# The head of the first FFN in a two-layer trunk, built another way

## The chip, the cores and the metric

The kernel runs on one core of one Trainium2 chip, alone. The metric is the device time of one execution in microseconds (us), taken as the median of three runs. An execution's profile gives a span, from the first to the last instruction of the core.

## What is computed

Six sublayers in a row (FFN, mixer, FFN, twice) update x, which has 256 rows of 1024. Each begins with a norm whose shift and scale come from a linear layer on c (`mod`), and the change touches the very first one and the first part of its FFN. Cut to that:

```python
c_act = jax.nn.silu(c)                                    # 1 x 1024
mod = (c_act @ mod_w[i] + mod_b[i]).reshape(B, 3, 3, 1024)
def adaln(x, g, shift, scale):
    return rmsnorm(x, g) * (1 + scale) + shift
def swiglu(h, w_in, w_out):                               # w_in: 1024 x 5632
    gate, up = jnp.split(h @ w_in, 2, axis=-1)
    return (jax.nn.silu(gate) * up) @ w_out
h = adaln(x, norm_g[i, 0], mod[:, 0, 0], mod[:, 0, 1])    # shift, scale
x = x + 0.5 * mod[:, 0, 2] * swiglu(h, ffn_w_in[i, 0], ffn_w_out[i, 0])
```

## The kernel before

Everything is float32. A product h @ w is done in three matmul passes per tile on TensorE: h and w are each split into a rounded high part and a rest (`hTh` and `hTl`, `hl[:, 0]` and `hl[:, 1]`), and high x high, high x rest and rest x high are added in PSUM. For a weight tile of 128 rows (one K tile, of 8) ScalarE makes the high part (a cast) and VectorE the rest (a subtraction); h stands transposed (1024 on partitions in 8 K tiles, 256 columns), and its two halves of 128 rows are t = 0 and 1.

**The head** (function `head`, lines 427 to 534) makes the first h and the first products with it: `g` (the first 1024 columns of the gate, four PSUM banks) and `u00a` (the first 512 columns of up, two banks). After it comes `u00b`, the next 512 columns of up, a plain `product`, then `g001` and the rest of the FFN. Shift (part 0) and scale (part 1) of layer 0 each need c_act times a 1024 x 1024 block of `mod_w`. The head does this in four blocks of 256 columns per part, 1 MB each (`hw`, or `spare`, which borrows a buffer that is not needed yet). Of the eight K slices of a block, `NPE` are multiplied on TensorE with `cb` as the stationary operand, that is c_act spread over all 128 columns, so that the result stands on every row; the others are summed on VectorE into `mb` (line 472), and a matmul with `ones` adds that sum (line 477). A matmul with a single row brings in the bias `mod_b` (line 462). Shift and scale are then rows: VectorE forms x * r * scale + shift in two steps (lines 485, 487), r being 1/rms of the row, TensorE transposes the block (line 494), and ScalarE and VectorE make `hTh` and `hTl`.

**Order.** Loads go out on the SP queue in the order of the code, as soon as their buffer is free; at most eight are on the way, since a load waits for the one eight places before it. SP stops at a load whose buffer is still read, and all later loads wait behind it. On the other engines a scheduler sorts the instructions by its own estimates of time; an engine then runs its list strictly in order. `hw` has two buffers (tag `mraw`), the transposed blocks and dummy results share two PSUM banks (tag `tr`).

## Time and profile before

| what | value |
| --- | --- |
| median of three runs (lowest, highest) | 1153.16 us (1152.34, 1154.13) |
| the profiled execution: time, span | 1151.26 us, 1149.5 us |
| busy: TensorE, its weight loads, VectorE, ScalarE | 98%, 82%, 72%, 51% |
| DMA, mean over the span | 244 GB/s |
| chain that ended last: TensorE, VectorE, ScalarE | 88%, 6%, 2% |

A float32 matmul shows as two records (passes) in the trace, one with the operands of the split products (float32r) as one. The busy time of TensorE is modelled from the starts of pipelined passes, so a gap between starts tells more than a duration does. "PEclk" is the clock that was granted to TensorE, as a share of its upper level; "<-" in brackets names what ended a wait.

### The profile page before, as it was taken

The page shows a single profiled execution, that of the slowest core. Times are in us where ns is not written, and L with a number is a line of the kernel's source. Part 1 is how long each engine was busy: PE and PEld are TensorE (multiplying, and loading weights), DVE is VectorE, ACT ScalarE, POOL GpSimd, SP SyncE. Part 2 cuts the span into 40 slices and gives each one's busy share as a digit, 9 for nine tenths or more (in the row PEclk, how much of TensorE's full clock was granted, in tenths as well). Part 3 has the DMA queues.
Part 4 walks back from the last instruction along what each step waited for, and adds up shares of the span by engine and source line. Part 5 has one row for each costly group of instructions (what it writes and reads, how often), then busy time and mean ns, then how long its engine had stood idle before and what let it go on. Part 6 is the DMA issues. An engine that isn't in the chain of part 4 may idle for free.

```text
span 1149.5 us, 14007 instructions
## 1 busy us (share of the span) xinstructions
PE 1125.9 (98%) x5381; PEld 943.8 (82%) x5381; DVE 828.0 (72%) x1008; ACT 590.8 (51%) x849; POOL 32.2 (3%) x42
## 2 busy tenths in 40 slices
PE   6999999999999999999999999999999999999997
PEld 5788998887878888888988788898877778889985
DVE  3887787845698788694678858577898877644653
ACT  3365454437555554554544546354457666544541
POOL 0000000010000000000000000000000000000000
PEclk9999999999999999999999999999999999999999
DMA  9787897547687685775778558487877555455640
GB/s 337 273 347 277 287 336 284 219 165 256 226 337 290 246 327 205 277 262 178 272 269 331 184 206 306 140 308 271 311 242 289 202 183 200 166 183 151 219 144 37
DMA packets 86538, 279.99 MB, mean 244 GB/s; under 512 B 4980, under 2 KB 15284, under 8 KB 86472
## 3 DMA queue, kind: packets, MB, share of 16 engines
q1 hardware_dynamic: 86472, 279.10, 68.5%
q8 instruction: 42, 0.69, 0.2%
q14 instruction: 24, 0.20, 0.1%
HBM read 278.01 MB, written 1.07 MB: 243 GB/s over the span
## 4 chain that ended last, share of the span: by engine, by line
PE 88%; DVE 6%; ACT 2%; DMA 1%; issue 1%; POOL 1%; SPq 0%; POOLq 0%; DVEq 0%; ACTq 0%
PE ps_o L201 27%; PE ps_g L201 19%; PE ps_u L201 19%; PE ps_v L201 5%; PE ps_gu L201 4%; PE ps_qk L201 3%; PE ta L386 2%; PE mps L132 1%; PE ps_vv L201 1%; PE hps L465 1%; DVE hl_g L180 1%; PE ps_u00b L201 1%; PE sv L609 1%; PE ps_u00a L201 1%; POOL rx L273 1%
## 5 line engine op out<-in xcount | busy, mean ns | idle before, releaser
L201 PE MATMUL ps_o<-hl_o,ahl 128*128 128x512 f32 x1440 | 333.9, 391 | 1.0 <-ACT ahl L342 1.0
L201 PEld LDWEIGHTS ps_o<-hl_o,ahl 128*128 128x128 f32 x1440 | 269.0, 188 | 56.3 <-ACT ahl L342 1.2
L201 PE MATMUL ps_g<-hl_g,hTh 128*128 128x512 f32 (+1 forms) x768 | 203.5, 375 | 0.7 <-ACT hTh L498 0.7
L180 DVE TENSOR_TENSOR hl_o<-raw_o,hl_o 128x1024 fp32r<-128x1024 f32 x120 | 145.7, 1222 | 53.8 <-ACT hl_o L179 53.2
L179 ACT CAST hl_o<-raw_o 128x1024 fp32r<-128x1024 f32 x120 | 125.6, 1055 | 112.2 <-PE ps_o L201 73.6
L201 PE MATMUL ps_u<-hl_u,hTh 128*128 128x512 f32 (+1 forms) x704 | 181.5, 369 | 0.0
L114 DVE SCALAR_TENSOR_TENSOR ma<-mw,cs,ma 128x1024 f32<-128x1024 f32 x128 | 163.8, 1280 | 13.4 <-DMA mw<-in_mod_w_dram 12.7
L201 PEld LDWEIGHTS ps_g<-hl_g,hTh 128*128 128x128 f32 x768 | 141.5, 189 | 21.7 <-ACT hTh L498 1.4
L180 DVE TENSOR_TENSOR hl_g<-raw_g,hl_g 128x1024 fp32r<-128x1024 f32 (+1 forms) x96 | 107.6, 1132 | 55.2 <-ACT hl_g L179 54.9
L201 PEld LDWEIGHTS ps_u<-hl_u,hTh 128*128 128x128 f32 x704 | 129.6, 188 | 17.6
L179 ACT CAST hl_g<-raw_g 128x1024 fp32r<-128x1024 f32 (+1 forms) x96 | 91.9, 980 | 100.4 <-PE ps_u L201 86.8
L180 DVE TENSOR_TENSOR hl_u<-raw_u,hl_u 128x1024 fp32r<-128x1024 f32 (+1 forms) x88 | 98.5, 1127 | 61.6 <-ACT hl_u L179 60.4
L201 PE MATMUL ps_g<-hl_g,hTl 128*128 128x512 f32 (+1 forms) x384 | 121.4, 377 | 0.0
L179 ACT CAST hl_u<-raw_u 128x1024 fp32r<-128x1024 f32 (+1 forms) x88 | 85.5, 974 | 61.0 <-PE ps_g L201 55.9
L201 PE MATMUL ps_u<-hl_u,hTl 128*128 128x512 f32 (+1 forms) x352 | 108.6, 369 | 0.0
L201 PEld LDWEIGHTS ps_g<-hl_g,hTl 128*128 128x128 f32 x384 | 71.4, 189 | 11.2 <-issue 1.3
L201 PEld LDWEIGHTS ps_u<-hl_u,hTl 128*128 128x128 f32 x352 | 65.4, 188 | 8.7
L201 PE MATMUL ps_gu<-hl_gu,hTh 128*128 128x512 f32 x192 | 55.0, 394 | 0.0
L201 PE MATMUL ps_v<-hl_v,hTh 128*128 128x512 f32 x192 | 54.2, 392 | 0.3 <-ACT hl_v L179 0.3
L180 DVE TENSOR_TENSOR hl_v<-raw_v,hl_v 128x1024 fp32r<-128x1024 f32 x24 | 28.9, 1220 | 27.3 <-ACT hl_v L179 27.3
L201 PEld LDWEIGHTS ps_v<-hl_v,hTh 128*128 128x128 f32 x192 | 35.8, 188 | 8.3 <-ACT hl_v L179 0.5
L201 PEld LDWEIGHTS ps_gu<-hl_gu,hTh 128*128 128x128 f32 x192 | 35.8, 188 | 7.1
(160 smaller groups left out, 1202.0 us busy)
## 6 DMA issues: line engine op xcount, KB each, us to landing
mw<-in_mod_w_dram SPq DMA_DIRECT2D x64, 1024.0 KB
raw_o<-in_ffn_w_out_dram SPq DMA_DIRECT2D x44, 1024.0 KB
raw_g<-in_ffn_w_in_dram SPq DMA_DIRECT2D x32, 1024.0 KB
raw_u<-in_ffn_w_in_dram SPq DMA_DIRECT2D x28, 1024.0 KB
raw_g<-in_ffn_w_in_dram SPq DMA_DIRECT2D x16, 768.0 KB
...
```

What stands on the lines that cost most here:

```text
L114: nc.vector.scalar_tensor_tensor(st["acc"], w[:, j, :], cs[:, k0 + j:k0 + j + 1], st["acc"], op0=ALU.mult, op1=ALU.add)
L132: nc.tensor.matmul(ps, lhs, hl[:, j, sl], start=j == 0, stop=j == 1)
L179: nc.scalar.copy(hl[:, 0, :w], r[:, kt % 2, :w])
L180: nc.vector.tensor_sub(hl[:, 1, :w], r[:, kt % 2, :w], hl[:, 0, :w].bitcast(F32))
L201: nc.tensor.matmul(ps[t, h][:, :cw], lhs(k, t)[p], hls[k][:, wp, o:o + cw], start=k == 0 and p == 0 and wp == 0, stop=k == nk - 1 and p == 1)
L273: nc.gpsimd.tensor_tensor(r, m, mhalf, op=ALU.pow)
L386: nc.tensor.transpose(ps[:, j * P:(j + 1) * P], src[:, j * P:(j + 1) * P], ident)
L465: nc.tensor.matmul(ps[part], cb[:, k, :], w[:, k, :], start=False, stop=k == KD - 1)
L609: nc.tensor.matmul(sv[:, sl], wsT[:, g, :], v[n][:, t, lo - n * D:hi - n * D], start=True, stop=True)
```

## The change

- Shift and scale are no longer spread over rows. The stationary operand is `cz`, 32 columns of which only the first holds c_act; eight K slices (or four, `HPE`) go to four strips of 32 output partitions, strip k mod 4 for slice k (`tile_position`). For blocks 3 and 4 VectorE adds the other four slices onto that PSUM tile. One matmul per 128 columns, with the summed tile as stationary operand and a single column of ones, sums over partitions and leaves shift and scale with their index on the partition (`columns`, `hv`).
- x, times r, is transposed at once (`xT`), before shift and scale are known. h is then one ScalarE instruction per K tile with scale and bias taken per partition (`acts_hi`), and its rest needs a second one and one on VectorE (`acts_lo`). `mod_b` and `norm_g` come in as 24 rows and are transposed in one go (`vrow`, `base`).
- The blocks are five (128, 128, 256, 256 and 256 columns), shift and scale side by side. Weights of `g` and `u00a` are loaded K tile by K tile, not in pairs, and x goes first in the queue.
- TensorE, VectorE and ScalarE keep the order of the code in the head (`manual_schedule`), with 33 dummy matmuls (`fill`) in it, 16 of them at the start.

```diff
-NPE = ((6, 5), (5, 2), (3, 1), (2, 1))
+BLOCKS = ((0, 128), (128, 128), (256, 256), (512, 256), (768, 256))
+HPE = (8, 8, 8, 4, 4)
...
+        def load(k):
+            for n, c0, w in (("g", 0, D), ("u", FF, 512)):
...
+                nc.sync.dma_start(raw[n][:, k % 2, :], w_in[k * P:(k + 1) * P, c0:c0 + w])
...
         def modulation(b):
...
+            n = 2 * BLOCKS[b][1]
+            ps = tr_bank(f"hps{b}")
+            for k in range(HPE[b]):
+                q = k % 4 * 32
+                nc.tensor.matmul(ps[q:q + 32, :n], cz[:, k, :], weight(b, k), start=k < 4,
+                                 stop=k >= HPE[b] - 4, tile_position=(0, q),
+                                 skip_group_check=True)
...
+        def gather(b):
...
+            if HPE[b] == KD:
+                nc.vector.tensor_copy(mb[:, :n], ps[:, :n])
+            prev = ps
+            for k in range(HPE[b], KD):
+                nc.vector.scalar_tensor_tensor(mb[:, :n], weight(b, k), cs[:, k:k + 1],
+                                               prev[:, :n], op0=ALU.mult, op1=ALU.add)
+                prev = mb
...
+        def columns(b):
+            ps, mb = sums[b]
+            for j in range(2 * BLOCKS[b][1] // P):
+                nc.tensor.matmul(ps[:, j:j + 1], mb[:, j * P:(j + 1) * P],
+                                 ones.bitcast(F32)[:, 0:1], start=True, stop=True)
+        def vectors(b):
...
+            nc.vector.tensor_add(v, sums[b][0][:, :2 * nj].rearrange("p (a j) -> p a j", a=2),
+                                 base[:, 0:2, k0:k0 + nj])
+            nc.vector.tensor_mul(v[:, 1, :], v[:, 1, :], base[:, 2, k0:k0 + nj])
...
+        def acts_hi(k):
+            sh, sc = hv[:, 0, k:k + 1], hv[:, 1, k:k + 1]
+            hi = hT["hi"][:, k, :]
+            nc.scalar.activation(hi, xT[k // 4][:, k % 4, :], AF.Identity, scale=sc, bias=sh)
+            less[k] = half_tile(f"hm{k}")[:, :S]
+            nc.scalar.activation(less[k], hi.bitcast(F32), AF.Identity, scale=-1.0, bias=sh)
+        def acts_lo(k):
+            nc.vector.scalar_tensor_tensor(hT["lo"][:, k, :], xT[k // 4][:, k % 4, :],
+                                           hv[:, 1, k:k + 1], less[k], op0=ALU.mult, op1=ALU.add)
...
+        def fill(n):
+            ps = tr_bank("fill")
+            for _ in range(n):
+                nc.tensor.matmul(ps, ones, ones[:, None, :].to_broadcast([P, 4, P]),
+                                 start=True, stop=True)
...
+        with tc.manual_schedule(engines={mybir.EngineType.PE, mybir.EngineType.DVE,
+                                         mybir.EngineType.Activation}):
+            fill(16)
...
+            modulation(0)
+            more(3)
+            gather(0)
+            cast(0, "g")
+            fill(2)
+            columns(0)
+            vectors(0)
+            acts_hi(0)
+            rest(0, "g")
+            acts_lo(0)
+            cast(0, "u")
+            rest(0, "u")
+            fill(4)
+            first(0)
+            modulation(1)
+            gather(1)
+            second(0, "g")
...
+            for k in range(2, KD, 2):
+                b = k // 2 + 2
+                first(k)
+                second(k, "g")
+                second(k, "u")
+                for n in "gu":
+                    cast(k + 1, n)
+                    rest(k + 1, n)
+                if b < len(BLOCKS):
+                    if k == 2:
+                        fill(2)
+                    modulation(b)
+                    gather(b)
+                first(k + 1)
+                second(k + 1, "g")
+                if b < len(BLOCKS):
+                    columns(b)
...
+                second(k + 1, "u")
```

`first(k)` is high x high of K tile k for g and u (six passes), `second(k, n)` the other two products (eight passes for g, four for u). `fetch(b)` loads a block in halves of 512 KB, two for blocks 0 and 1, four for the others.

On SP, the start of the kernel before (`hw` and `spare` are blocks of mod_w, `raw_g` and `raw_u00a` pairs of K tiles of the FFN's weights):

```order
L453 DMA hw01_99<-in_mod_w_dram 128x8x256
L505 DMA row10_90<-in_mod_b_dram 1x512
L453 DMA hw00_105<-in_mod_w_dram 128x8x256
L508 DMA x0_69<-in_x_dram 128x1024
L508 DMA x1_70<-in_x_dram 128x1024
L509 DMA gn0_98<-in_norm_g_dram 128x1024
L173 DMA raw_g000_0_166<-in_ffn_w_in_dram 128x2x1024
L173 DMA raw_u00a_0_171<-in_ffn_w_in_dram 128x2x512
L453 DMA spare_97<-in_mod_w_dram 128x8x256 x2
L173 DMA raw_g000_2_262<-in_ffn_w_in_dram 128x2x1024
```

and of the changed kernel:

```order
L553 DMA x0_69<-in_x_dram 128x1024
L553 DMA x1_70<-in_x_dram 128x1024
L452 DMA hw00_93<-in_mod_w_dram 128x8x128 x2
L557 DMA vrow_92<-in_mod_b_dram 8x128 x2
L557 DMA vrow_92<-in_norm_g_dram 8x128
L461 DMA rawg0_99<-in_ffn_w_in_dram 128x1024
L461 DMA rawu0_101<-in_ffn_w_in_dram 128x512
L452 DMA hw10_103<-in_mod_w_dram 128x8x128 x2
L461 DMA rawg0_99<-in_ffn_w_in_dram 128x1024
L461 DMA rawu0_101<-in_ffn_w_in_dram 128x512
L452 DMA spare_87<-in_mod_w_dram 128x4x256 x4
L461 DMA rawg2_112<-in_ffn_w_in_dram 128x1024
```

x moved from behind 2 MB of mod_w to the front, and the first block is half as large.

On TensorE, from the first transposes of the kernel before (`htr`: a block of h; `hps`: a block of shift or scale; `ps_g`, `ps_u00a`: the products):

```order
L494 MATMUL htr0_159<-ident_73,hh0_154 128x128 x2
L462 MATMUL hps11_184<-row10_90,ones_78 128x256
L494 MATMUL htr0_159<-ident_73,hh0_154 128x128 x2
L462 MATMUL hps10_189<-row00_94,ones_78 128x256
L201 MATMUL ps_g000_00_213<-hl_g000_0_168,hTh_85 128x512
```

and in the changed kernel from the transposed bias to the same product:

```order
L592 MATMUL vrow_204<-ident_73,vrow_92 128x24
L549 MATMUL fill_208<-ones_78 128x512 x2
L484 MATMUL hps0_211<-hw00_93,cz_88 32x256 x8
L549 MATMUL fill_235<-ones_78 128x512 x2
L503 MATMUL hps0_211<-ones_78,mb0_220 128x1 x2
L549 MATMUL fill_250<-ones_78 128x512 x4
L532 MATMUL ps_g00000_122<-hl_g0_233,hTh_85 128x512
```

The transposes now stand ahead of the first block's modulation, and the products follow it after two matmuls of one column.

On VectorE, behind the head, in the kernel before (`u00b` and `g001`: rests of the next weights; `ma002`: sums for the next modulation; `pr`: gate times up; `ahl`: rests of the FFN's inner activations):

```order
L404 TENSOR_TENSOR pr00_506<-ps_u00a_00_229,sg00_498 128x512
L404 TENSOR_TENSOR pr10_514<-ps_u00a_10_233,sg10_502 128x512
L180 TENSOR_TENSOR hl_u00b_6_593<-raw_u00b_6_591,hl_u00b_6_593 128x512
L180 TENSOR_TENSOR hl_u00b_7_602<-raw_u00b_6_591,hl_u00b_7_602 128x512
L114 SCALAR_TENSOR_TENSOR ma002_558<-mw0022_605,cs_71,ma002_558 128x1024
L343 TENSOR_TENSOR ahl0_1292<-act00_497,ahl0_1292 128x512
```

and in the changed kernel:

```order
L407 TENSOR_TENSOR pr00_563<-ps_u00a0_126,sg00_555 128x512
L407 TENSOR_TENSOR pr10_571<-ps_u00a1_127,sg10_559 128x512
L117 SCALAR_TENSOR_TENSOR ma002_615<-mw0020_618,cs_71,ma002_615 128x1024
L183 TENSOR_TENSOR hl_u00b_4_630<-raw_u00b_4_628,hl_u00b_4_630 128x512
L117 SCALAR_TENSOR_TENSOR ma002_615<-mw0020_618,cs_71,ma002_615 128x1024
L183 TENSOR_TENSOR hl_u00b_5_639<-raw_u00b_4_628,hl_u00b_5_639 128x512
L183 TENSOR_TENSOR hl_u00b_6_650<-raw_u00b_6_648,hl_u00b_6_650 128x512
L183 TENSOR_TENSOR hl_u00b_7_659<-raw_u00b_6_648,hl_u00b_7_659 128x512
```

Four rests of u00b and two sums, not two rests, now stand behind the gated products.

## Rows read from the trace of the kernel before

**Rows 1.** The page: busy us, share and instructions of each engine.

```profile
PE 1125.9 (98%) x5381; PEld 943.8 (82%) x5381; DVE 828.0 (72%) x1008; ACT 590.8 (51%) x849; POOL 32.2 (3%) x42
```

**Rows 2.** The chain that ended last: start us, us, what.

```profile
506.34 13.60 PE ps_g L201 x60
```

**Rows 3.** Timeline, TensorE: first g, last u00a, first u00b (start us, us, instruction).

```profile
20.69 1.22 PE L201 MATMUL ps_g<-hl_g,hTh 128*128 128x512 f32 x4
...
69.53 0.39 PE L201 MATMUL ps_u00a<-hl_u00a,hTl 128*128 128x512 f32 x1
69.75 0.62 PE L201 MATMUL ps_u00b<-hl_u00b,hTh 128*128 128x512 f32 x2
```

**Rows 4.** Stretches: busy us (and starts) by engine, PEclk, DMA share, GB/s.

```profile
10.00:12.00 2.00, 2.00 (x7) 1.40 (x5) 0.48 (x1) 1.23 (x4) 0.00 (x0) 1.00 1.03 412
18.00:20.00 2.00, 0.67 (x4) 0.20 (x2) 0.68 (x1) 1.30 (x2) 0.00 (x0) 1.00 1.09 348
20.00:30.00 10.00, 9.93 (x36) 7.86 (x37) 6.25 (x11) 3.14 (x6) 0.00 (x0) 0.83 1.07 369
42.00:44.00 2.00, 2.00 (x11) 1.69 (x10) 1.83 (x5) 0.06 (x1) 0.00 (x0) 1.00 0.00 0
242.00:243.00 1.00, 1.00 (x6) 0.81 (x6) 0.00 (x0) 0.00 (x0) 0.00 (x0) 1.00 1.06 305
```

**Rows 5.** Waits of the SP queue up to 60 us: total, times, longest.

```profile
SPq L453 <- DVE mb L472: 14.0, 1, 14.0
```

**Rows 6.** Timeline, TensorE: passes of the modulation and transposes.

```profile
29.68 2.11 PE L465 MATMUL hps<-spare,cb 128*128 128x256 f32 x9
47.65 0.60 PE L494 MATMUL htr<-ident,hh 128*128 128x128 f32 x4
```

**Rows 7.** Timeline, TensorE, attention: matmuls with 64 output columns, then a transpose.

```profile
921.99 0.66 PE L733 MATMUL ov<-pT,vs 128*64 128x256 f32 x4
922.47 0.40 PE L734 MATMUL ov<-pT,vs 128*64 128x128 f32 x4
922.69 0.65 PE L733 MATMUL ov<-pT,vs 128*64 128x256 f32 x4
...
923.49 0.33 PE L707 MATMUL tp<-ident,lg 128*128 128x128 f32 x1
```

**Rows 8.** Timeline, ScalarE at the start: what waits for loads, and x's squares.

```profile
6.75 0.51 ACT L468 ACTIVATE mb<-hw,cs 128x256 f32<-128x256 f32 x1 [4.12 <-DMA hw<-in_mod_w_dram]
9.67 0.51 ACT L468 ACTIVATE mb<-hw,cs 128x256 f32<-128x256 f32 x1 [2.41 <-DMA hw<-in_mod_w_dram]
10.95 0.63 ACT L264 ACTIVATE junkx<-x 128x512 f32<-128x512 f32 x1 [0.77 <-DMA x<-in_x_dram]
...
12.85 0.61 ACT L264 ACTIVATE junkx<-x 128x512 f32<-128x512 f32 x1
```

**Rows 9.** Groups by line and shape: count, busy us, mean ns.

```profile
L282 ACT CAST hTh<-tr_h 128x512 fp32r<-128x512 f32 x20 | 11.6, 586 | 29.5 <-PE tr_h L280 29.1
L331 DVE TENSOR_SCALAR o<-o,rfin 128x512 f32<-128x512 f32 x2 | 1.0, 486 | 1.5 <-POOL rfin L273 1.5
L468 ACT ACTIVATE mb<-hw,cs 128x256 f32<-128x256 f32 x5 | 2.4, 504 | 6.5 <-DMA hw<-in_mod_w_dram 6.5
```

**Rows 10.** Timeline, VectorE: a mean square, and the step that waits for r.

```profile
220.09 0.16 DVE L268 SCALAR_TENSOR_TENSOR mx<-ssx,ssx 128x1 f32<-128x1 f32 x1
220.92 1.42 DVE L295 SCALAR_TENSOR_TENSOR h<-h,rx,bc 128x512 f32<-128x512 f32 x2 [0.66 <-POOL rx L273]
```

**Rows 11.** Groups by line and shape, VectorE: rests (wide, narrow), two sums.

```profile
L180 DVE TENSOR_TENSOR hl_o<-raw_o,hl_o 128x1024 fp32r<-128x1024 f32 x120 | 145.7, 1222 | 53.8 <-ACT hl_o L179 53.2
L180 DVE TENSOR_TENSOR hl_u00b<-raw_u00b,hl_u00b 128x512 fp32r<-128x512 f32 x8 | 5.2, 684 | 1.8 <-ACT hl_u00b L179 1.8
L295 DVE SCALAR_TENSOR_TENSOR h<-h,rx,bc 128x512 f32<-128x512 f32 x20 | 14.1, 749 | 4.6 <-POOL rx L273 4.5
L114 DVE SCALAR_TENSOR_TENSOR ma<-mw,cs,ma 128x1024 f32<-128x1024 f32 x128 | 163.8, 1280 | 13.4 <-DMA mw<-in_mod_w_dram 12.7
```

More of the change, by code (lines that the diff above doesn't have):

```diff
@@ L501, in head @@
-        fetch(0, 1)
-        for part in (1, 0):
-            for h in range(2):
-                o = part * D + h * 512
-                nc.sync.dma_start(row[part, h], mod_b[0:1, o:o + 512])
-        fetch(0, 0)
+        spare = new_act("spare").rearrange("p a b -> p (a b)")
+        cz = pool.tile([P, D], F32, tag="macc", name="cz", bufs=2)[:, :KD * 32]
+        cz = cz.rearrange("p (k n) -> p k n", k=KD)
+        nc.gpsimd.memset(cz, 0.0)
+        g, u, hws, sums, raw, hls = {}, {}, {}, {}, {}, {}
@@ new lines, in fetch @@
+        def fetch(b):
+            c0, cw = BLOCKS[b]
+            per = 1024 // cw
+            for k0 in range(0, KD, per):
+                n = HOME[b, k0]
+                if n is None:
+                    w = pool.tile([P, 2 * D], F32, tag="mraw", name=f"hw{b}{k0}", bufs=2)
+                else:
+                    w = spare[:, n * 2 * D:(n + 1) * 2 * D]
+                w = w.rearrange("p (k a n) -> p k a n", a=2, n=cw)
+                for part in range(2):
+                    o = part * D + c0
+                    nc.sync.dma_start(w[:, :, part, :], src[:, k0:k0 + per, o:o + cw])
+                hws[b, k0] = w
@@ new lines, in more @@
+        def more(b):
+            fetch(b)
+            load(2 * b - 2)
+            load(2 * b - 1)
+        more(2)
+        xT = [pool.tile([P, 4, S], F32, tag="bc", name=f"xT{h}", bufs=3) for h in range(2)]
+        base = stat.tile([P, 3, KD], F32, tag="base", name="base", bufs=1)
+        hv = stat.tile([P, 2, KD], F32, tag="hv", name="hv", bufs=1)
+        prod = {"g": {(t, h): acc_bank(f"ps_g000{t}{h}") for t in range(NT) for h in range(2)},
+                "u": {(t, 0): acc_bank(f"ps_u00a{t}") for t in range(NT)}}
```

189 lines of the change are left out of this document (102 added, 87 removed).

## The prediction

> **What bounds the kernel now.** I read the page first, then the chain of waits, the timeline of the first 90 us, and the stretches and waits of the loads in it. TensorE is busy for 98% of the span [rows 1]. A busy TensorE is not yet a full one, so I took the chain: in it 60 passes of 512 columns follow each other in 13.60 us, 0.227 us each [rows 2], and this is the pace nearly everywhere behind the head. So the kernel behaves like a list of TensorE work that begins once the first h exists: what the head saves in TensorE time, the end saves too, unless a later stage can't follow.
>
> The head: the first pass of g starts at 20.69, the last of u00a at 69.53, the first of u00b at 69.75 [rows 3], 49.06 us. What fills them: g and u00a are 8 K tiles x 18 passes = 144 passes x 0.227 = 32.7. In the same stretch 24 float32 matmuls for shift and scale (14 with `cb`, six that add VectorE's sum, four for the bias) take two passes each, and a pass costs 2.11 / 9 = 0.23 [rows 6]: 10.9. Twelve transposes take about 0.11 each (four in 0.60, with the last one's way through the array in it) [rows 6]: 1.3. That is 44.9. Between 20 and 30 us the granted clock is 0.83 on average [rows 4], after a stretch of two us with only four starts in it; 10 us x 0.17 is 1.7 us lost. The rest, 2.5, are waits. So TensorE is nearly full from 20.7 on, and two things can be won: the start, and the 12 us of shift, scale and transposes.
>
> One thing is not the bound there: SP stands still for 14.0 us at one load [rows 5], and no byte moves from 42 to 44 us [rows 4], yet TensorE has its 11 starts in those two us. The gap costs nothing now; it would in a head that is shorter.
>
> **The start of the products.** Before, the first MB of mod_w (rows of 1 KB) wakes ScalarE at 6.75, the second at 9.67, 2.92 later, and half an MB of x (rows of 4 KB) at 10.95, 1.28 later [rows 8]. So bytes begin to move near 6.75 - 2.92 = 3.8. With x in front, its halves land at 5.1 and 6.4. The first block follows, 1 MB in runs of 512 bytes. No load of the head before has such runs; bounds are 348 GB/s in a stretch of 1 KB rows and 305 in one of the load `ws`, whose source has runs of 128 floats [rows 4], so 3.0 to 3.4 us. It lands near 9.7, and it will not matter, because the chain of x is longer:
> - Four squares take 12.85 + 0.61 - 10.95 = 2.5 us [rows 8], 5.1 to 7.7. VectorE's list has both mean squares ahead of the scaling; the second is done at 7.9, when r of the first half is long there (0.83 from a mean square to its user [rows 10]). Scaling 512 columns costs 0.49 [rows 9]: 8.4. Four transposes 0.60: 9.0.
> - Two copies out of PSUM at 0.59 [rows 9]: 10.2. The second frees the bank for the other half's transposes, 10.8; its first copy ends at 11.4, then the bias is transposed and copied (0.3), two dummies run (0.45): 12.2.
> - Modulation of block 0: 1.0 (below), 13.2; its way out and a copy of 256 columns, 0.7 (0.5 for ScalarE's instruction of that size [rows 9], taken for VectorE's): 13.9. Two matmuls of one column, four passes priced as transposes, 0.6: 14.5. Two tiny VectorE steps at 0.16 [rows 10]: 14.8. The activation that makes h's high part, 0.50 [rows 9]: 15.3. The first product starts at 15.4 and not at 20.69: **5.3 us earlier**. The copies, the dummies and r are all on this path, so each could cost 1 more; the landing of x could give 0.5.
>
> **TensorE's list from there.**
> - The 144 passes stay: 32.7.
> - Modulation of blocks 1 to 4. This is the open price: nothing in the trace uses strips of 32 columns. The nearest rows are the attention's matmuls with 64 output columns, which go to two halves of the array. Two heads there are four passes of 256 and four of 128 columns. One after the other they would need 4 x 0.23 + 4 x 0.11 = 1.36; from 921.99 to the next group at 922.69 it is 0.70 [rows 7]. So the halves run side by side, float32 too, and each needs its own passes and 0.06. I take four strips to do the same. Block 1: two matmuls per strip, two passes each of 256 columns, 4 x 0.227 + 0.06 = 0.97. Block 2: the same with 512 columns, 1.87. Blocks 3 and 4: one matmul per strip, 0.97 each. Sum 4.8. The lower bound is this; the upper is one after the other, 16 x 0.227 + 16 x 0.454 + 2 x 8 x 0.454 = 18.2.
> - Going from strips to the whole array and back: the transpose behind the second group starts at 923.49 and not at 922.69 + 0.70 = 923.39 [rows 7], 0.1; eight times 0.8.
> - One-column matmuls: 14 for blocks 1 to 4, two passes at 0.11 (the weights have to go in): 3.1. It could be half or twice that.
> - Six dummies behind the first product: 1.4. The 27 ahead of it run in waits or are counted in the start.
> - Transposes are gone, since x was turned before.
>
> That is 42.8. Then waits: behind each of the four gathers TensorE has columns, two small VectorE steps and 0.50 of ScalarE before the next K tile's product can start; in between stand second(0, "u") and its like, four passes or 0.9 us, and one to three dummies. This covers all but 0.2 to 0.4 each time, and the cast for u, behind two activations, is late by 0.2 more. With a weight load that is not hidden after each such wait I take 3.0 for all (1.5 to 4.5). The gathers of blocks 3 and 4 are four VectorE steps of 0.75 [rows 11], 3.0, behind 14 passes of 3.2: hidden, with nothing to spare.
>
> Loads: at 2.92 per MB in 1 KB rows, 1.28 per half MB of g and 0.64 for u, blocks 1 to 4 land near 14.8, 22.7, 32.6 and 42.4, and the last K tile near 46. TensorE asks for the blocks at about 16.8, 25, 35 and 46. So margins are 2 to 3 us, and eight loads on the way are 3 MB, enough. The dummies and strips move nothing on SP or GpSimd; the buffers that the last two blocks wait for are read by modulations 0 to 2, long done, so the 14 us stop on SP goes.
>
> Head's end: 15.4 + 42.8 + 3.0 = 61.2, against 69.75: **8.6 us less**. The profiled execution took 1151.26 (its span 1149.5 and 1.8 around it) and would take 1142.7; the median of the runs is 1153.16, 1.9 above it, and I forecast against that: **1144.6**.
>
> **What comes late next.** Behind the head VectorE has, before g001 can start: eight rests of u00b at 0.684, two products and two rests of the same width, four sums at 1.28 and one rest at 1.222 [rows 11], 5.5 + 1.4 + 1.4 + 5.1 + 1.2 = 14.6. It gets to them near 57 (block 4's chain and 5 us of rests) and has to wait about 1.5 for the gate: 73. TensorE wants g001 after 48 passes and 8 transposes, 61.2 + 11.8 = 73.0. There is no slack, but a late sum costs 1.28 once and not per K tile, because afterwards VectorE needs 1.22 for a K tile whose 12 passes take 2.7.
>
> **Rivals.**
> - *VectorE gives part back* behind the head: two sums late and a load behind them, up to 3 us: 1147. For: no slack, and the new list puts the two sums of the first pair between u00b's rests. Against: VectorE is freed of the head's 31 partial sums. 0.15.
> - *Only two strips at a time*: the modulations double, +4.8 and +1.0 in the start, of which waits take 0.5: gain 3.3, 1149.9. For: two is all that the trace shows. 0.08.
> - *Strips run one after the other*, the one that ends slower: 18.2 for 4.8 and 3.6 for 1.0 in block 0, 16 us more, of which waits cover 1: the head ends near 76, 6.4 later than before: 1159.6. It decides once all five modulations cost 14 us and not 5.8. For: 0.70 is seen with 64 columns alone. Against: the same rows. 0.09. The Trainium skill, TensorE: Matmul & The Clock Gate, section Part 3, has a rule that speaks for this rival: a weight load overlaps a running matmul only where the row group differs, and the strips here share all rows. By that rule loads and passes would alternate, to about that time; the trace does not agree, as its halves share their rows and still take 0.70.
> - *Nothing comes of it*: x or the blocks land as late as today, each wait moves to a load, within 2 us of 1153. 0.06.
>
> **Numbers.** The forecast has 0.62, with 1141 to 1147 as its own range: upward one or two spells at the lower clock like that of 20 to 30 us (1.7 each, likelier here because TensorE has only scattered work before 15) and a wait sum of 4.5; downward cheaper one-column matmuls and waits of 1.5. With the first two rivals 0.85 lies in 1141 to 1150. Faster by over 0.2% (2.3 us, about what a measurement of this kernel can tell from no change) 0.85, within it 0.06, slower 0.09.
>
> **What would show it.** The first pass of g near 15.4 and the first of u00b near 61; the eight matmuls of block 2 done in about 1.9 us, their starts in groups of four; no stop of SP over 3 us; blocks 3 and 4 landed before TensorE asks; PEclk at 1.00 from 16 on; in g001 no TensorE gaps that wait for VectorE. I am wrong if block 2 takes 3.7 or 7 us, if the first g is later than 18, or if TensorE waits for loads.

## The result, and the profile after

| | kernel before | changed kernel |
| --- | --- | --- |
| median of four runs each, on one chip | 1152.75 us | 1144.67 us |
| lowest, highest | 1151.22, 1154.13 | 1144.19, 1144.84 |
| profiled execution: time, span | 1151.26, 1149.5 us | 1144.84, 1143.0 us |
| first pass of g, first of u00b | 20.69, 69.75 | 16.67, 62.18 |
| busy: TensorE, weight loads, VectorE, ScalarE | 98%, 82%, 72%, 51% | 98%, 82%, 72%, 52% |

The ratio of after to before is 0.9929, with a 95% interval of 0.9914 to 0.9945: 8.1 us faster, between the medians. The two profiled executions are only 6.4 apart, since the one of before lies 1.5 below its median; what follows compares the traces and keeps that in mind.

The page of the changed kernel, where it answers [rows 1] (the counts are matmul passes and instructions):

```profile
PE 1125.2 (98%) x5429; PEld 938.3 (82%) x5429; DVE 820.5 (72%) x988; ACT 593.5 (52%) x853; POOL 33.0 (3%) x43
```

There are 48 more TensorE records and almost the same busy time: a share of busy time says nothing of this change. What moved is when things start. TensorE's timeline of the changed kernel, from its first instruction to the first product, then block 2 and the end of the head (start us, us, engine, line, operation, tiles, count, idle time ahead of it and what ended that). `fill` are the dummies, `htr` x turned, `hps` the modulations, first in strips (`cz`) and then the one-column matmuls (`ones,mb`); line numbers up to the head are 3 higher than before, so L204 is what L201 was:

```profile
1.20 6.20 PE L549 MATMUL fill<-ones 128*128 128x512 f32 x16 [1.20 <-POOL ones L90]
8.72 1.11 PE L585 MATMUL htr<-ident,xr 128*128 128x128 f32 x8 [1.32 <-DVE xr L582]
10.05 0.96 PE L549 MATMUL fill<-ones 128*128 128x512 f32 x3 [0.22 <-DVE xr L582]
10.85 1.03 PE L585 MATMUL htr<-ident,xr 128*128 128x128 f32 x8
12.12 0.24 PE L592 MATMUL vrow<-ident,vrow 24*128 24x24 f32 x1 [0.24 <-ACT xT L587]
12.64 0.73 PE L549 MATMUL fill<-ones 128*128 128x512 f32 x2 [0.28 <-DVE base L593]
13.30 1.07 PE L484 MATMUL hps<-hw,cz 128*32 128x256 f32 x16
14.30 0.73 PE L549 MATMUL fill<-ones 128*128 128x512 f32 x2
14.92 0.61 PE L503 MATMUL hps<-ones,mb 128*128 128x1 f32 x4
15.39 1.17 PE L549 MATMUL fill<-ones 128*128 128x512 f32 x4
16.67 1.20 PE L532 MATMUL ps_g<-hl_g,hTh 128*128 128x512 f32 x4
...
26.53 1.92 PE L484 MATMUL hps<-spare,cz 128*32 128x512 f32 x16
28.38 0.72 PE L532 MATMUL ps_u00a<-hl_u,hTh 128*128 128x512 f32 x2
...
30.23 0.94 PE L549 MATMUL fill<-ones 128*128 128x512 f32 x3
31.45 1.21 PE L532 MATMUL ps_g<-hl_g,hTh 128*128 128x512 f32 x4 [0.28 <-ACT hTh L520]
...
62.18 0.61 PE L204 MATMUL ps_u00b<-hl_u00b,hTh 128*128 128x512 f32 x2
```

Against [rows 3] the first product comes 4.02 us earlier and u00b 7.57 earlier. From the first product to u00b it is 45.5 us, not 49.06. Block 2, 16 float32 passes of 512 columns, is over after 28.38 - 26.53 = 1.85 us. A pass of 256 columns takes 0.23 [rows 6], so one of 512 takes some 0.46 and 16 of them 7.4 one after another; 1.85 is four, which means that the four strips work side by side. At 31.45, behind three dummies, stands the only wait of the head behind the first product that shows as idle time.

Stretches of the changed kernel (busy us and starts by engine, PEclk, DMA share, GB/s), and the longest stop of the SP queue up to 100 us (total, times, longest):

```profile
22.00:24.00 2.00, 2.00 (x9) 1.25 (x8) 1.87 (x5) 1.62 (x3) 0.00 (x0) 1.00 1.05 374
54.00:56.00 2.00, 2.00 (x9) 1.44 (x9) 1.56 (x4) 1.97 (x5) 0.00 (x0) 1.00 0.09 34
58.00:60.00 2.00, 2.00 (x11) 1.65 (x10) 2.00 (x4) 1.31 (x3) 0.00 (x0) 1.00 0.20 29
```

```profile
SPq L176 <- DVE hl_u L471: 10.9, 2, 9.6
```

The spell of half clock that [rows 4] show between 20 and 30 us is gone. The stop of SP is not: it moved from 42 us to the load of u00b's weights (9.6 us for a buffer that `hl_u` still reads), and little is moved in 54 to 56 and 58 to 60 us (34 and 29 GB/s); TensorE starts nine and eleven passes there all the same.

### The profile page after: what moved, and what is told of

Its sections match the earlier page's. It is cut to its first block, busy times and chain, and to the rows that moved or that the text cites. A ratio compares the mean times of both kernels' runs of the same rounds, so it can differ in the third digit from the quotient of the medians.

```text
span 1143.0 us, 14125 instructions
## 1 busy us (share of the span) xinstructions
PE 1125.2 (98%) x5429; PEld 938.3 (82%) x5429; DVE 820.5 (72%) x988; ACT 593.5 (52%) x853; POOL 33.0 (3%) x43
## 4 chain that ended last, share of the span: by engine, by line
PE 85%; DVE 7%; DMA 3%; ACT 2%; issue 1%; POOL 1%; SPq 0%; POOLq 0%; DVEq 0%; ACTq 0%
PE ps_o L204 23%; PE ps_u L204 19%; PE ps_g L204 18%; PE ps_gu L204 6%; PE ps_v L204 5%; DMA mw<-in_mod_w_dram 3%; PE ps_qk L204 3%; PE ps_g L532 2%; PE ta L389 2%; DVE ma L117 1%; PE mps L135 1%; PE sv L750 1%; PE ps_u00b L204 1%; DVE hl_g L183 1%; PE ps_u00a L532 1%
## 5 line engine op out<-in xcount | busy, mean ns | idle before, releaser
L204 PE MATMUL ps_o<-hl_o,ahl 128*128 128x512 f32 x1440 | 334.1, 391 | 1.0 <-ACT ahl L345 1.0
L204 PEld LDWEIGHTS ps_o<-hl_o,ahl 128*128 128x128 f32 x1440 | 269.1, 188 | 56.3 <-ACT ahl L345 1.2
L204 PE MATMUL ps_g<-hl_g,hTh 128*128 128x512 f32 (+1 forms) x704 | 183.4, 371 | 0.0
L204 PE MATMUL ps_u<-hl_u,hTh 128*128 128x512 f32 (+1 forms) x704 | 181.5, 369 | 0.0
L204 PEld LDWEIGHTS ps_u<-hl_u,hTh 128*128 128x128 f32 x704 | 129.6, 188 | 17.6
L204 PEld LDWEIGHTS ps_g<-hl_g,hTh 128*128 128x128 f32 x704 | 129.2, 188 | 17.5 <-ACT hTh L285 0.2
L183 DVE TENSOR_TENSOR hl_g<-raw_g,hl_g 128x1024 fp32r<-128x1024 f32 (+1 forms) x88 | 97.6, 1124 | 50.8 <-ACT hl_g L182 50.5
L182 ACT CAST hl_g<-raw_g 128x1024 fp32r<-128x1024 f32 (+1 forms) x88 | 83.3, 974 | 94.8 <-PE ps_u L204 84.1
L204 PE MATMUL ps_g<-hl_g,hTl 128*128 128x512 f32 (+1 forms) x352 | 110.3, 372 | 0.0
L204 PE MATMUL ps_u<-hl_u,hTl 128*128 128x512 f32 (+1 forms) x352 | 108.6, 369 | 0.0
L204 PEld LDWEIGHTS ps_u<-hl_u,hTl 128*128 128x128 f32 x352 | 65.4, 188 | 8.7
L204 PEld LDWEIGHTS ps_g<-hl_g,hTl 128*128 128x128 f32 x352 | 65.0, 188 | 9.1 <-issue 0.6
L204 PE MATMUL ps_gu<-hl_gu,hTh 128*128 128x512 f32 x192 | 55.0, 394 | 0.0
L204 PE MATMUL ps_v<-hl_v,hTh 128*128 128x512 f32 x192 | 54.2, 392 | 0.3 <-ACT hl_v L182 0.3
L183 DVE TENSOR_TENSOR hl_v<-raw_v,hl_v 128x1024 fp32r<-128x1024 f32 x24 | 28.8, 1221 | 22.7 <-ACT hl_v L182 22.7
L204 PEld LDWEIGHTS ps_v<-hl_v,hTh 128*128 128x128 f32 x192 | 35.8, 188 | 8.4 <-ACT hl_v L182 0.5
L204 PEld LDWEIGHTS ps_gu<-hl_gu,hTh 128*128 128x128 f32 x192 | 35.8, 188 | 7.1
```

The source lines that it names most:

```text
L182: nc.scalar.copy(hl[:, 0, :w], r[:, kt % 2, :w])
L183: nc.vector.tensor_sub(hl[:, 1, :w], r[:, kt % 2, :w], hl[:, 0, :w].bitcast(F32))
L204: nc.tensor.matmul(ps[t, h][:, :cw], lhs(k, t)[p], hls[k][:, wp, o:o + cw], start=k == 0 and p == 0 and wp == 0, stop=k == nk - 1 and p == 1)
```

## The experiments

The ratio is to the kernel before in runs on the same chip, with its 95% interval. First g, first u00b and the span belong to the profiled execution.

| kernel | first g | first u00b | span | median us | ratio |
| --- | --- | --- | --- | --- | --- |
| changed kernel | 16.67 | 62.18 | 1143.0 | 1144.67 | 0.9929 (0.9914 to 0.9945) |
| full_width | 18.76 | 76.23 | 1156.9 | 1158.58 | 1.0054 (1.0039 to 1.0068) |
| sched | 24.91 | 78.30 | 1158.9 | 1157.86 | 1.0045 (1.0029 to 1.0062) |
| no_fill | 16.44 | 64.02 | 1144.7 | 1146.56 | 0.9947 (0.9935 to 0.9959) |
| fill_start | 14.87 | 62.61 | 1147.7 | 1146.70 | 0.9950 (0.9937 to 0.9964) |
| fill_trim | 15.49 | 60.95 | 1141.9 | 1144.15 | 0.9927 (0.9915 to 0.9939) |
| x_late | 21.81 | 67.28 | 1149.6 | 1150.27 | 0.9977 (0.9967 to 0.9986) |
| before_x_first | 25.05 | 73.43 | 1152.8 | 1155.51 | 1.0026 (1.0011 to 1.0041) |
| pairs | 16.29 | 61.80 | 1141.9 | 1144.47 | 0.9934 (0.9919 to 0.9949) |
| hpe8 | 16.54 | 63.61 | 1146.0 | 1145.82 | 0.9941 (0.9923 to 0.9959) |
| sums_later | 16.24 | 61.74 | 1142.9 | 1144.62 | 0.9933 (0.9918 to 0.9948) |
| short_start | 14.17 | 60.17 | 1142.1 | 1143.44 | 0.9920 (0.9908 to 0.9932) |
| short_sums | 14.17 | 60.72 | 1140.8 | 1142.65 | 0.9910 (0.9895 to 0.9926) |

First g, first u00b and the span come from the trace of one execution. The first two resolve 0.4 us or so: sums_later has the head of the changed kernel, and both its times lie 0.43 to 0.44 lower. The stretch between the two is firmer (45.51 and 45.50 us). A median moves by 1 us from one set of runs to the next. So the head's steps are judged by the first two columns, the whole by the last.

### Are the strips what makes a modulation cheap?

```diff
-        cz = pool.tile([P, D], F32, tag="macc", name="cz", bufs=2)[:, :KD * 32]
+        cz = pool.tile([P, D], F32, tag="macc", name="cz", bufs=2)
...
-                nc.tensor.matmul(ps[q:q + 32, :n], cz[:, k, :], weight(b, k), start=k < 4,
-                                 stop=k >= HPE[b] - 4, tile_position=(0, q),
+                nc.tensor.matmul(ps[:, :n], cz[:, k, :], weight(b, k), start=k == 0,
+                                 stop=k == HPE[b] - 1)
```

> The changed kernel, but c_act stands in a stationary operand of all 128 columns (one used, 127 zero), so that the eight or four matmuls of a block go one after another into the whole array; the result is the same. My theory, that the strips are what makes a modulation cheap: 16 passes of 0.227 instead of 1.0 us in blocks 0 and 1, 16 of 0.454 instead of 1.9 in block 2, 8 of 0.454 instead of 1.0 in blocks 3 and 4, so 21.8 us for 5.9. That is 16 more, of which waits take one: u00b starts near 77 instead of 62.2, and the time is 1159 us (1157 to 1161). Rival, that the gain came from the earlier start and the dropped bias, sum and transpose matmuls, and the strips are worth little: within 2 us of the changed kernel, 1145 to 1147.

TensorE's timeline of full_width, blocks 0, 2 and 3:

```profile
12.88 3.61 PE L483 MATMUL hps<-hw,cz 128*128 128x256 f32 x16
...
30.75 7.03 PE L483 MATMUL hps<-spare,cz 128*128 128x512 f32 x16
...
45.55 3.59 PE L483 MATMUL hps<-spare,cz 128*128 128x512 f32 x8
```

The same passes, one after another: 3.6 for 1.0, 7.0 for 1.9, 3.6 for 1.0. u00b starts 14.05 later and the time is 13.9 longer, slower than the kernel before. So the strips carry more than the whole gain; without them the new head would have been a loss. This is the prediction's third rival, made to happen, and its price (1159.6) was right to 1 us.

The Trainium skill, TensorE: Matmul & The Clock Gate, section Part 3: Packing small matmuls, says that a weight load overlaps running matmuls only where the row group differs. The strips here all use the same 128 rows, and the trace does not agree: 1.85 us for 16 passes, 7.03 without strips. The Trainium skill, TensorEngine Tiling (Array Packing), section Tiling Modes, lists 128x32 as four tiles that load weights and multiply in parallel, and with that the trace agrees.

### What are the dummies worth?

Three kernels; the label stands behind the lines that each has.

```diff
         def fill(n):
+            return                      # no_fill
+            if n != 16:                 # fill_start
+                return
...
-                if t == 0:              # fill_trim
-                    fill(3)
...
-            fill(2)                     # fill_trim
             modulation(0)
```

> The changed kernel without its 33 dummy matmuls; the order of all other instructions stays. Theory one, that the dummies hold the clock: TensorE starts at 8.7 us at the lower level, has only scattered work until the first product, and runs 3 to 5 us of products at half speed, 1.5 to 2.5 lost there and 1 in the transposes and the first modulation; about 1 is won since three and two dummies leave the path to the first product. 1146 us (1145 to 1148), with a granted clock under 1.00 behind 16 us. Theory two, that the dummies only stand in the way: first product 1 us earlier, clock as before, 1143.7.

> The changed kernel with the first 16 dummies alone; the 17 later ones are gone. Theory one, that the later ones are needed too: the clock rises at 6 us and falls again after the scattered stretch from 8 to 16 us, as it fell in the kernel before at 21.8 us for 3.4 us after such a stretch: 1.7 lost, 0.9 won on the path to the first product, about 1145.5 (1144.7 to 1146.5). Theory two, that the first 16 suffice: clock 1.00 all along, 0.9 won, 1143.8.

> The changed kernel without the three dummies between the two halves' transposes and the two ahead of the first modulation, five of 33, those that stand on the path to the first product. They take 0.2 to 0.4 us of the first and 0.66 of the second place. Theory one, that the clock holds without them: first product at 15.7 instead of 16.67, the head's end as much earlier, 1143.8 us (1143.4 to 1144.2). Theory two, that the stretch becomes too scattered: the clock falls for a while near 13 to 18 us and 1 to 1.7 us are lost, 1145 to 1145.5.

Stretches of no_fill at the first products and behind the largest wait, then the same of fill_start (PEclk is the third number from the end):

```profile
16.00:18.00 2.00, 1.56 (x4) 1.28 (x5) 1.85 (x3) 1.97 (x4) 0.00 (x0) 0.50 1.04 371
18.00:20.00 2.00, 2.00 (x20) 0.96 (x18) 0.16 (x1) 0.38 (x1) 0.00 (x0) 0.67 1.09 348
...
32.00:34.00 2.00, 1.70 (x5) 1.34 (x6) 1.91 (x3) 1.94 (x5) 0.00 (x0) 0.74 1.09 382
34.00:36.00 2.00, 2.00 (x6) 1.55 (x5) 1.20 (x3) 1.80 (x3) 0.00 (x0) 0.50 1.04 402
```

```profile
14.00:16.00 2.00, 1.13 (x3) 0.93 (x4) 1.85 (x4) 1.62 (x3) 0.00 (x0) 0.67 1.12 355
16.00:18.00 2.00, 2.00 (x9) 1.09 (x11) 0.60 (x1) 0.90 (x1) 0.00 (x0) 0.50 1.05 364
...
32.00:34.00 2.00, 2.00 (x6) 1.61 (x6) 1.19 (x3) 1.97 (x4) 0.00 (x0) 0.50 1.05 377
```

Theory one held, and it was two spells and not one: the clock falls to half at the first products and again near 32 us, behind the wait for block 2's chain. What they cost can be read against the changed kernel. From the first product to that of K tile 1, no_fill takes 7.38 us (16.44 to 23.82) where the changed kernel takes 6.31 with one dummy of 0.23 in it: 1.3 lost. From the product behind block 2's chain (32.30, there 31.45) to u00b it takes 31.72 where the changed kernel takes 30.73 with two dummies of 0.55: 1.5 lost. The three dummies at 30.23 cost nothing, since they run in a wait: from the one-column matmuls ahead of them to the next product it is 2.04 us with them and 2.03 without. So no_fill loses 2.8 to the clock, wins 0.8 of dummies behind the first product and 0.23 at the start; u00b is 1.84 later. Fill_start loses 1.5 and 1.5, wins 0.8 and 1.8; u00b is 0.43 later. I had one spell there, and its time lies just above what I had written. It is that of no_fill all the same, with runs spread from 1144.92 to 1149.58. The profiled one is the slowest of them and loses most of that far behind the head: TensorE waits 1.57 us at 866.60, where the changed kernel has no such wait, and 2.26 at 927.02, where that has 1.0.

So the first 16 dummies bring 1.4 us at u00b (62.61 against 64.02; with them the 16 transposes take twice 1.1 us, in no_fill 3.76), though nothing in the medians. The twelve others that fill_trim keeps, most of them at 14 to 16 and at 30 us, keep the clock up. The five that fill_trim takes away are not among them: PEclk stays at 1.00, and the first product comes 1.18 earlier, u00b 1.23. They had stood on the path. That this makes the whole faster too (the profiled execution took 1143.64 against 1144.84, but the median is only 0.5 lower) can't be told from these runs.

### Does x's chain set the start, and does the end follow it?

Two kernels, one made from the changed kernel and one from the kernel before; the loop that loads x is moved, so it is gone from its old place.

```diff
         vrow = half_tile("vrow")[:3 * KD, :P]
         fetch(0)
+        for t in range(NT):                                    # x_late: behind the block
+            nc.sync.dma_start(x_sb[t], x[0, t * P:(t + 1) * P, :])
...
+        for t in range(NT):                                    # before_x_first, ahead of
+            nc.sync.dma_start(x_sb[t], x[0, t * P:(t + 1) * P, :])   # the block's loads
         fetch(0, 1)
```

> The changed kernel, but the first block of mod_w (1 MB) is loaded ahead of x, not behind it; nothing else moves. Theory, that the chain from x (squares, 1/rms, scaling, transposes) sets the start and the head's end follows it: x lands 3.0 to 3.3 us later (1 MB in runs of 512 bytes), the first product comes near 19.8 instead of 16.67, u00b as much later, 1147.8 us (1147 to 1148.5; 1.7 more if the clock falls in the longer wait). Rival, that the first block's arrival or TensorE's list sets the start: within 0.5 us of the changed kernel, 1144.2 to 1145.2.

> The kernel before with x moved to the front of the queue, as the change has it, and nothing else. Theory, that the early x pays only because the change made the work on x independent of shift and scale: here h needs both 1 MB loads of the first block, which now land 2.6 us later; the first product comes 1 to 2.6 us later than 20.69, 1153 to 1155 us. Rival, that the queue's order alone brings the earlier start: first product at 16 to 18, 1148 to 1150 us.

x_late, TensorE's timeline and a stretch (PEclk is the third number from the end), then before_x_first, ScalarE's waits for the two halves of the block and TensorE's timeline:

```profile
12.13 1.97 PE L585 MATMUL htr<-ident,xr 128*128 128x128 f32 x8 [5.69 <-DVE xr L582]
...
21.81 1.21 PE L532 MATMUL ps_g<-hl_g,hTh 128*128 128x512 f32 x4
```

```profile
14.00:16.00 2.00, 2.00 (x7) 1.61 (x7) 0.00 (x0) 0.58 (x1) 0.00 (x0) 0.50 1.13 355
```

```profile
9.64 0.51 ACT L468 ACTIVATE mb<-hw,cs 128x256 f32<-128x256 f32 x1 [1.74 <-DMA hw<-in_mod_w_dram]
12.64 0.51 ACT L468 ACTIVATE mb<-hw,cs 128x256 f32<-128x256 f32 x1 [2.49 <-DMA hw<-in_mod_w_dram]
...
17.46 4.08 PE L465 MATMUL hps<-hw,cb 128*128 128x256 f32 x12
...
25.05 1.20 PE L201 MATMUL ps_g<-hl_g,hTh 128*128 128x512 f32 x4 [0.68 <-ACT hTh L498]
```

In x_late the transposes come 3.41 later (x lands that much later), TensorE stands for 5.69 us, and from 12.13 to 17.7 us it runs at half clock, which adds 1.7: the first product is 5.14 later, u00b 5.10, the time 5.6 (1150.27, where I had 1147 to 1148.5 and 1.7 more with the clock down). So the head's end follows its start one to one. Before_x_first has the early x and gains nothing from it: the second half of the block wakes ScalarE at 12.64, not at 9.67 [rows 8], the first product comes 4.36 later and the time is 2.7 longer. I had 1 to 2.6 there; the rest is that TensorE starts 3 us later and so runs its second 12 passes in 4.08 us, much of that at the lower clock, which it did in 2.75 before:

```profile
7.66 4.32 PE L465 MATMUL hps<-hw,cb 128*128 128x256 f32 x10
...
13.07 2.75 PE L465 MATMUL hps<-hw,cb 128*128 128x256 f32 x12
```

Those are the same two groups in the kernel before. The early x pays only because the change took shift and scale out of its chain.

### The fixed order

```diff
-        with tc.manual_schedule(engines={mybir.EngineType.PE, mybir.EngineType.DVE,
-                                         mybir.EngineType.Activation}):
+        if True:
```

> The changed kernel without the fixed order in the head: TensorE, VectorE and ScalarE take the scheduler's order, all instructions are the same. It puts casts of the weights ahead of x's copies and ahead of the first activation on ScalarE, and block 1's modulation ahead of the first product. Theory, that an order that waits for loads in the chain from x costs the start: the cast of K tile 1 waits for its load until 16.6 and stands ahead of the first activation, first product near 18.4 instead of 16.67, 1146.4 us (1145.5 to 1148). Rival, that the order matters little, since TensorE's list is what bounds the head: 1144.2 to 1145.2.

ScalarE and TensorE of sched, in the start and at a later K tile, and two stretches:

```profile
12.34 1.04 ACT L467 CAST hl_g<-rawg 128x1024 fp32r<-128x1024 f32 x1 [2.94 <-DMA rawg<-in_ffn_w_in_dram]
...
13.93 0.66 PE L585 MATMUL htr<-ident,xr 128*128 128x128 f32 x4 [2.79 <-ACT xT L587]
...
24.91 1.08 PE L532 MATMUL ps_g<-hl_g,hTh 128*128 128x512 f32 x4
...
49.73 1.05 PE L503 MATMUL hps<-ones,mb 128*128 128x1 f32 x8
52.89 2.07 PE L532 MATMUL ps_g<-hl_g,hTh 128*128 128x512 f32 x4 [2.10 <-ACT hTh L520]
```

```profile
15.00:20.00 5.00, 4.75 (x22) 1.99 (x23) 1.02 (x4) 1.41 (x2) 0.00 (x0) 0.50 1.08 360
20.00:25.00 5.00, 5.00 (x26) 2.84 (x27) 1.89 (x5) 1.52 (x3) 0.00 (x0) 0.53 1.08 364
```

Both theories were far off: 1157.86, not 1146.4. The direction was right (a cast that waits for its weights stands ahead of x's second copy on ScalarE, and TensorE stands 2.79 us behind it), the price was not. Behind that wait the clock is at half from about 14.5 to 24.7 us, all through dummies and modulations (0.95 in 10 to 15 us, then 0.50 and 0.53), and the first product comes 8.24 later. Block 1's modulation stands ahead of it now, too (1.9 us at half clock). Then the one-column matmuls stand behind, not ahead of, the last four passes of a K tile, so nothing covers the chain to the next h: TensorE waits 1.06, 2.10 and 1.57 us for `hTh` before three K tiles, with two more spells of half clock behind the waits. u00b comes 16.12 later (in an execution of 1160.86, the slowest of five). Taken alone the fixed order is worth 13 us, nearly as much as the strips: without either of the two the rebuilt head is slower than the one before.

### Single tiles or pairs, and four slices on VectorE

```diff
-                nc.sync.dma_start(raw[n][:, k % 2, :], w_in[k * P:(k + 1) * P, c0:c0 + w])
+                if k % 2 == 0:                                            # pairs
+                    nc.sync.dma_start(raw[n], w_in[k * P:(k + 2) * P, c0:c0 + w].rearrange(
+                        "(k p) n -> p k n", p=P))
...
-HPE = (8, 8, 8, 4, 4)
+HPE = (8, 8, 8, 8, 8)                                                     # hpe8
```

> The changed kernel with the weights of g and u00a loaded in pairs of K tiles, one transfer for two, as the kernel before does, in the same places of the queue. Theory, that the blocks and K tiles land 2 to 3 us ahead of their use: a pair lands at most 1.9 us behind its first single tile, so nothing waits, 1144.7 us (1144.2 to 1145.3). Rival, that the first tile of a pair comes too late: TensorE waits up to 1.9 us at the first product or at block 1, 1145.5 to 1147.

> The changed kernel with all eight K slices of blocks 3 and 4 on TensorE, instead of four there and four as sums on VectorE. Theory, that the head is TensorE's list and the sums are hidden behind products: two blocks x 0.95 us more, u00b at 64.0 instead of 62.18, 1146.5 us (1145.8 to 1147.2). Rival, that VectorE's 3.0 us of sums stand on the path to the next K tile: they go, and the time stays or falls, 1143.7 to 1144.8.

Pairs are as good: u00b at 61.80, 1144.47. Loading tile by tile is a part of the change without an effect that these runs resolve. In hpe8 the head takes 63.61 - 16.54 = 47.1 us and not 45.5: 1.6 of the 1.9 that TensorE was given, so VectorE's four sums each of the two blocks were hidden but for 0.3 in all.

### Where some of the head's gain goes

The changed kernel, VectorE and TensorE at the end of the first FFN (`y`, `x`, `h`: the residual steps; `ma`: sums for a later modulation; `tr_h`: the next sublayer's transposes):

```profile
209.20 2.61 DVE L117 SCALAR_TENSOR_TENSOR ma<-mw,cs,ma 128x1024 f32<-128x1024 f32 x2 [1.93 <-DMA mw<-in_mod_w_dram]
...
216.92 0.66 PE L283 MATMUL tr_h<-ident,h 128*128 128x128 f32 x4 [0.67 <-DVE h L298]
```

This looked like the rival of late sums at another place: two sums wait for a load, the residual behind them, TensorE behind that.

```diff
         def piece(k0):
...
+                c = cs
+                if (i, s, part) == (0, 1, 2) and k0 == 4:
+                    c = stat.tile([P, KD], F32, tag="cs2", name="cs2", bufs=1)
+                    nc.vector.scalar_tensor_tensor(c, x_sb[0][:, 512:512 + KD], 0.0, cs,
+                                                   op0=ALU.mult, op1=ALU.add)
...
-                        st["acc"], w[:, j, :], cs[:, k0 + j:k0 + j + 1], st["acc"],
+                        st["acc"], w[:, j, :], c[:, k0 + j:k0 + j + 1], st["acc"],
```

> The changed kernel with its head untouched. In the changed kernel's trace two of VectorE's sums for a later modulation stand between the residual steps at the end of the first FFN; they wait until 209.2 us for a load of mod_w, and TensorE has a gap of 1.06 us behind them at 215.9. Here these two sums read a copy of c_act that is made from the new x, so that they stand behind the residual steps. Theory, that this wait is where 0.9 us of the head's gain is given back: the gap goes, the transposes of the next sublayer start at 215.9 or 1 us earlier than 216.92, 1143.7 us (1143.2 to 1144.2). Rival, that something else is late there (the squares and 1/rms behind the residual, or the next load, which now waits for the later sums): within 0.4 us of the changed kernel, 1144.3 to 1145.3.

```profile
209.52 0.69 DVE L312 TENSOR_TENSOR y<-ps_o,bc 128x512 f32<-128x512 f32 x1 [2.66 <-PE ps_o L209]
...
212.25 1.28 DVE L122 SCALAR_TENSOR_TENSOR ma<-mw,cs,ma 128x1024 f32<-128x1024 f32 x1
213.46 0.15 DVE L276 SCALAR_TENSOR_TENSOR mx<-ssx,ssx 128x1 f32<-128x1 f32 x1
...
216.11 0.66 PE L288 MATMUL tr_h<-ident,h 128*128 128x128 f32 x4 [0.51 <-DVE h L303]
```

The time is the rival's, but the theory is not settled by it. Without the sums `y` waits for TensorE itself, until 209.52, 2.2 us earlier than in the changed kernel (211.73), and the wait for the load is off the path. But the moved sums now stand on it. From that `y` to h it takes 5.8 us here (to 215.30) and 4.4 there (to 216.11): the squares on ScalarE end at 212.2, and the mean square `mx` runs 1.3 us later, behind the first of the sums. So the transposes come 0.8 earlier, of which this execution had 0.43 at its first product already. The idle time shrinks from 0.67 to 0.51, and the time is the same. What the path would take with both sums behind it no run here shows.

### A shorter start

```diff
-                    ps = tr_bank(f"htr{t}{h}")
+                    ps = htr[t, h]          # banks of g, idle until the first product
...
-                if t == 0:
-                    fill(3)
...
-            fill(2)
             modulation(0)
```

and the 24 rows of bias and norm loaded ahead of the first block; short_sums has the edit of sums_later besides.

> The changed kernel with a shorter start: the five dummies ahead of the first modulation are gone, the four groups of transposes of x go to four PSUM banks of the products (idle until then) instead of waiting for ScalarE's copies in two, and the 24 rows of bias and norm are loaded ahead of the first block. If the start is the chain squares, scaling, transposes, block 0's modulation, gather, columns, vectors, activation: transposes end at 11.0, modulation at 12.2, first product at 14.5 (14.2 to 15.0) instead of 16.67, u00b at 60 to 60.5, 1142.6 us (1142.0 to 1143.4). Rival one, that the first block lands too late for that (after 11.5): first product at 15.2 or later, 1143.5. Rival two, that the loads of the later blocks become the bound, since TensorE now asks 2 us earlier and the margins were 2 to 3: u00b after 61, 1144.

> The short start (no dummies on the path, x's transposes into the products' banks, bias rows ahead of the first block) together with the later sums. If both theories hold, the two gains add, since the short start's trace has a gap of 1.17 us at the same place: 1142.3 us (1141.7 to 1143.0). Rival, that an earlier head only waits longer for loads further on: 1143.2 to 1144.2, as the short start alone.

short_start, TensorE's timeline:

```profile
8.66 2.04 PE L586 MATMUL htr<-ident,xr 128*128 128x128 f32 x16 [0.76 <-DVE xr L583]
...
14.17 1.20 PE L532 MATMUL ps_g<-hl_g,hTh 128*128 128x512 f32 x4
...
16.44 1.07 PE L484 MATMUL hps<-hw,cz 128*32 128x256 f32 x16 [0.48 <-DMA hw<-in_mod_w_dram]
```

The first product comes at 14.17, 2.5 earlier, and for the first time TensorE waits for a load in the head (0.48 for block 1): u00b is 2.01 earlier. The time is 1143.44, at the upper end of what the theory gave: 1.2 less by the medians, so that about 0.8 of the 2.0 would be lost behind the head, less than these runs resolve. Short_sums runs 1142.65, its four runs between 1141.82 and 1142.85, all below the fastest of the changed kernel (1144.19); against before it is 0.9910. It has the lowest median of this study, but its interval overlaps those of the changed kernel and of short_start, so the 2.0 and 0.8 us between the medians are not settled. Its head is not the shorter one (u00b at 60.72 against 60.17, with a second wait for a load, 0.30 us for block 2). What its execution gains it gains behind the head, and that this comes from the later sums is not shown.

## Why the prediction was right, and where it was not

The forecast was 1144.6 and the time is 1144.67. That is closer than its steps were: three of them (the start, what is given back behind the head, and the step from the profile to the median) are off by 1 to 2 us, and the errors cancel. That it met the time to 0.1 us is luck; that the time lies in the range is not.

- **What bounds the kernel** was right. TensorE's list begins at the first h; moving that beginning moved the end of the head one to one in x_late and fill_trim.
- **The start** was mis-sized: 15.4 predicted, 16.67 measured, 4.0 us won and not 5.3. x, the squares and r came within 0.3; from modulation 0 to the first product it is 16.67 - 13.30 = 3.4 against 3.2. What failed is the step in between, the transposes of the second half at 10.2 and modulation 0 at 12.2. They are at 10.85 and 13.30: three dummies of 0.8 us in all stand between the halves, and the next two wait for the copy of the bias (`base`) and then take 0.66. The prediction had 0.45 for dummies there, and said that each could cost 1 more. Fill_trim, without the five, has its first product at 15.49.
- **TensorE's list** was right term by term. Modulations 1.0, 1.85, 1.0 and 1.0 against 0.97, 1.87, 0.97 and 0.97; one-column matmuls about 3.0 against 3.1. From the first product to u00b 45.5, predicted 42.8 + 3.0 = 45.8. The price of the strips, the one open price, came from attention rows with two halves of the array [rows 7]; four strips behave like two halves, and full_width shows what the other answer would have been.
- **Waits and clock**: PEclk is at 1.00 behind the first rise at 6 us, as the sign said. The prediction counted the six dummies behind the first product as 1.4 us on TensorE's list and named no gain of dummies. They take 0.8 there, since three of them run in a wait, and no_fill shows that without dummies the head loses 2.8 us of clock behind its first product. The kernel before lost 1.7 in this way (10 us at 0.83), so about half of the 3.5 us by which the stretch from first g to u00b is shorter now is the clock, which the prediction has in its account of before; in the new list it stands only as a risk.
- **Loads**: TensorE never waits for one in the head, and there was enough room even for pairs. But the landing times, worked out from [rows 8], were too early: in short_start block 1 ends a wait at 16.44, where the prediction had 14.8, and in short_sums block 2 at 25.93, where it had 22.7. The changed kernel asks for them at 18.39 and 26.53, so its margins were 2 us and less, not 2 to 3. The sign "no stop of SP over 3 us" was wrong: the prediction had asked only who holds the buffers of the blocks, not those of u00b's weights behind them. It cost nothing, like the stop of 14 us before.
- **Behind the head** g001 starts right behind u00b, at 74.14 where the prediction had 73.0 from a head 1 us shorter; VectorE kept up. That rival did not come. Yet the lead does shrink, in steps: it is 7.57 us at u00b, 7.44 at the second up product (104.25 before, 96.81 after), 6.65 behind the first FFN's end (the first product of `ps_v`, 226.34 and 219.69), 7.49 again at the start of gmlp's gate, where the kernel before waits 1.78 us and the changed one 0.81, 6.65 at the third sublayer and 6.5 by the spans. The rows of both kernels are below. Of the 0.84 lost in the second half of gmlp, 0.50 are two waits for VectorE that only the changed kernel has (0.18 at 344.20, 0.32 at 440.38). But all this is one execution against one. By the same sum, the lead at u00b less that of the span, pairs and short_sums give back 0.4, the changed kernel 1.1, sums_later 1.4, short_start 2.2 and hpe8 2.6, though they run the same program behind the head, but for the two moved sums. So 1 us given back is no fixed price of the change. What sets it in one execution stays open.
- **From the profile to the median**: by the two traces the change is worth 6.4 us and the forecast of 8.6 was 2 too large (1.0 in the head, 1.1 behind it). Between the medians it is 8.1. I had added 1.9 us to my sum, since the profiled execution of before lay that much below its median; that of the changed kernel lies 0.2 above its own. The runs of before reach from 1150.9 to 1155.5 over this study, so the profile of one execution is a poor zero for a change of 8 us. The forecast met the time because it was made between medians; had the medians been 6.4 apart like the profiles, it would have been 1.7 off, inside the range.

The gate's start and the third sublayer's transposes, before and then after:

```profile
322.76 0.59 PE L609 MATMUL sv<-v,wsT 128*128 128x192 f32 x2 [1.78 <-DVE gp L611]
...
447.03 0.66 PE L280 MATMUL tr_h<-ident,h 128*128 128x128 f32 x4
```

```profile
315.27 0.59 PE L750 MATMUL sv<-v,wsT 128*128 128x192 f32 x2 [0.81 <-DVE gp L752]
...
440.38 0.66 PE L283 MATMUL tr_h<-ident,h 128*128 128x128 f32 x4 [0.32 <-DVE h L298]
```

## What to carry to other kernels

Where a matmul has one useful column, four strips of 32 side by side give four results in the time of one, in float32 too; price it from any row in which two halves of the array already run. An order written by hand around a chain is worth pricing as a part of its own: one cast that waits for its weights, put ahead of the chain's copy, made TensorE stand for 2.8 us, and some ten us at half clock followed. And dummies belong where TensorE would otherwise stand ahead of dense work, not in the chain that it waits for.

## What the runs showed of the chip

- A stop can cost more behind it than itself. In sched TensorE stood 2.79 us and was then at the lower level (0.50, 1.2 GHz) for about 10 us although it had starts all along (22 in one stretch of 5 us); in x_late, after 5.69 us of standing, it was there for 5.6 us; in no_fill and fill_start, behind waits of 1.08 to 1.15 us, each spell cost 1.3 to 1.5 us. With three or four dummies in those waits the changed kernel stayed at 1.00.
- The column PEclk does not show the level before its first recorded rise: it reads 1.00 from 10 to 12 us in [rows 4], while the ten passes from 7.66 to 11.98 (shown with before_x_first) take 0.43 us each, and the same kind 0.23 later [rows 6]. At the start the durations tell the clock, not the column.
